# Gate and up projection computed as one pair, with seven block products in place of eight for three of eight k-tile pairs

## The chip, the cores and the metric

The kernel runs on one core of a Trainium2 chip. The metric is device microseconds for one execution of the whole program. TensorE (PE in the profile) does the matmuls into PSUM, VectorE (DVE), ScalarE (ACT) and GpSimd (POOL) do the rest, and SyncE (SP) issues nearly all DMAs. Each engine runs its own instructions in a fixed order and waits on semaphores for the others.

## The reference, cut to what matters

Two layers over 256 tokens of width 2048: a gated linear attention layer and a differential attention layer, each followed by the same feed-forward block. The change touches the feed-forward block and how the residual `x` is kept while it runs.

```
def swiglu(h, w_gate_up, w_down):                 # h: 256 x 2048
    gate, up = jnp.split(h @ w_gate_up, 2, axis=-1)   # 2048 x (2 * 5632)
    return (jax.nn.silu(gate) * up) @ w_down          # 5632 x 2048
x = x + rmsnorm(mix, post_mix_g[i])
f = swiglu(rmsnorm(x, pre_ffn_g[i]), ffn_w_gate_up[i], ffn_w_down[i])
x = x + rmsnorm(f, post_ffn_g[i])
```

Everything is float32.

## The kernel before, in words

**Matmuls.** A float32 operand is split into a rounded `hi` part and a remainder `lo`, and a product of 128 x 128 by 128 x 512 is three matmuls, hi by hi, hi by lo and lo by hi (`mm_act`, lines 220 to 222). The stationary operand is 128 columns of one half of the tokens (b = 0 or 1), the moving operand 512 weight columns.

**Weights.** They come in units of 128 x 1024 floats (512 KB): two k-tiles by 512 columns. `weight_stream` lists every unit in the order of use. `load` issues the DMA of one into a ring of 4 `raw` buffers (SP queue, line 174). `convert` makes `hi` by a copy on ACT (line 185) and `lo` by a subtraction on DVE (line 188), into rings of 9 buffers. `take` hands a unit to the matmuls, `free` returns it, and `pump` converts and loads ahead as far as the rings allow, so that DVE stands up to 9 units ahead of PE.

**Chunks.** `chunk_act` computes 512 output columns for 256 tokens: 8 units, two accumulators in PSUM (one for each half of the tokens), 12 matmuls per unit. PSUM has 8 banks; the pool `acc` has six and the pool `tp` (for transposes) two. Of 11 column chunks of the feed-forward block each has a gate chunk and an up chunk; gate ends in a SiLU on ACT (line 684), up in a multiply on DVE (line 687), and `split_T` transposes the result through `tp` (line 289) and splits it into `gT` (lines 291, 292). The 11 chunks go in groups of 3, 4 and 4; after a group, four down chunks accumulate into `f`.

**Order.** Python code with deferred steps (`defer`, `tick`) writes a program, and the framework's scheduler then fixes each engine's order from its own estimate of when each instruction becomes ready.

Of the kernel before, what the change touches and what calls it, by code (L numbers as in the profile page):

```python
# [11 lines left out]
F32 = mybir.dt.float32  # L12
# [24 lines left out]
LAMBDA_INIT = 0.8 - 0.6 * math.exp(-0.3 * 1)  # L37
FF_GROUPS = ((0, 1, 2), (3, 4, 5, 6), (7, 8, 9, 10))
SKEW = 7
CHAIN = (3, 4, 5, 6)  # L40
NRAW, NRING = 4, 9


def weight_stream():
    out = []

    def chunk(name, n, ns=8, s0=0):
        out.extend((name, (n, s0 + s)) for s in range(ns))

    def block(name, n):  # L50
        out.extend((name, (n, s)) for s in range(2))

    def ffn(i):
        for grp in FF_GROUPS:
            for c in grp:
                chunk(f"w_gu{i}", c)
                chunk(f"w_gu{i}", 11 + c)
# [24 lines left out]
    return out  # L82


class Split:

# [11 lines left out]
    def lo(self, kt, sl=slice(None)):  # L98
        return self.part(kt, 1, sl, 1)[:, 0, :]

    def both(self, kt):
        return self.tiles[kt // 8][:, kt % 8, :, :].rearrange("p w t -> p (w t)")


class Trunk:
    def __init__(self, ctx, tc, t):
# [12 lines left out]
        self.later = []  # L119
        self.stream = weight_stream()  # L120
        self.subs = {}
        self.raws = {}
# [48 lines left out]
    def load(self):  # L171
        name, idx = self.stream[self.n_dma]
# [3 lines left out]
        self.n_dma += 1  # L176

    def convert(self):
        nc = self.nc
        n = self.n_conv  # L180
        if self.n_dma == n:
            self.load()
        raw = self.raws.pop(n)
        hi = self.ring.tile([P, 1024], F32R, tag="hi", name=self.uid("hi"), bufs=NRING)
        nc.scalar.copy(hi, raw)  # L185
        lo = self.ring.tile([P, 1024], F32R, tag="lo", name=self.uid("lo"), bufs=NRING)
        eng = nc.gpsimd if n in self.pool_lo else nc.vector
        eng.tensor_tensor(out=lo, in0=raw, in1=hi.bitcast(F32), op=ALU.subtract)  # L188
        self.subs[n] = (hi, lo)
        self.n_conv += 1  # L190

    def pump(self):
        n = len(self.stream)
        while self.n_conv < min(n, self.n_free + NRING, self.n_take + self.cap):
            self.convert()
            while self.n_dma < min(n, self.n_conv + NRAW):
                self.load()

    def take(self, name, idx):
        n = self.n_take  # L200
        assert self.stream[n] == (name, idx), (self.stream[n], name, idx)
        self.n_take += 1
# [21 lines left out]
    def chunk_act(self, aT, w, n, ns, evac, s0=0, head=0, tail=0, hook=None):  # L224
# [32 lines left out]
        evac(1, ps[1])  # L257

    def block_w(self, aT, w, n, evac):
# [55 lines left out]
    def gain(self, vec, c):  # L315
        g = self.hs.tile([P, C], F32, tag="gain", name=self.uid("gain"), bufs=3)
        self.nc.sync.dma_start(g, vec[:, c * C : (c + 1) * C].partition_broadcast(P))
        return g
# [217 lines left out]
    def gla(self, gp, hT, rs):  # L536
        nc, t = self.nc, self.t
        self.wf = gp.tile([GATE_RANK, GLA_DK], F32, tag="wf", name="wf")
# [4 lines left out]
        s3 = self.whole(3, [P, 8, C], "gla_qk")  # L543

        def r_chunk(h, hook=None):
# [127 lines left out]

    def ffn(self, fp, hT, rs, gi, wgu, wd, post, after, name, side=None):
        nc = self.nc
        f = self.whole(5, [P, 2, D], name)
        ss = [self.stat(), self.stat()]
        for gidx, grp in enumerate(FF_GROUPS):
            gT = self.pair(gi, f"{name}_gT{gidx}")
            for i, c in enumerate(grp):  # L680
                sg = fp.tile([P, 2, C], F32, tag="sg", name=self.uid("sg"), bufs=2)

# [7 lines left out]

                first = gidx == 0 and i == 0
                if side and gidx == 1 and i == 0:
                    self.defer(8, side)
                self.chunk_act(hT, wgu, c, 8, evac_gate, head=SKEW if first else 0)
                self.chunk_act(hT, wgu, 11 + c, 8, evac_up)
# [5 lines left out]
                self.defer(3, gate_T)  # L701
            last = gidx == len(FF_GROUPS) - 1
            for c in range(4):
                g = self.gain(post, c) if last else None

                def evac(b, ps):
# [5 lines left out]
                    if last:  # L712
                        self.square(fc, ss[b][:, c : c + 1])
                        fg = fp.tile([P, C], F32, tag="fg", name=self.uid("fg"), bufs=2) if c == 3 else fc
                        nc.vector.tensor_tensor(out=fg, in0=fc, in1=g, op=ALU.mult)
                        if c == 3:
                            fgs = [f[:, b, i * C : (i + 1) * C] for i in range(3)] + [fg]
                            after(b, self.add_norm(fgs, b, ss[b]))

                self.chunk_act(  # L720
                    gT, wd, c, 2 * len(grp), self.urgent(evac) if last and c == 3 else evac, s0=2 * grp[0], tail=SKEW if last and c == 3 else 0
                )

    def diff_stages(self, dp, oT, q, kT, v, h):
# [60 lines left out]
        def normed():  # L785
            ctx["og"] = []
            for b, (o, ss) in enumerate(ctx["o"]):
                og = dp.tile([P, SEQ], F32, tag=f"og{b}", name=f"og{h}_{b}")
                nc.vector.scalar_tensor_tensor(
# [29 lines left out]
    def run(self):  # L819
# [5 lines left out]
        with tc.tile_pool(name="gla", bufs=1) as gp:  # L825
            oT = self.gla(gp, hT, rs)
            hT = self.pair(0, "h_ffn0")
            rs = []
            self.proj_out(
                oT, "gla_w_out", t["post_mix_g"][0:1],  # L830
                self.norm_to(hT, 1, rs, "rs_ffn0_"), "f_mix0",
            )

        x_dram = self.dram.tile([2, P, D], F32, tag="x_dram", name="x_dram")
        hkv, rs_kv = [], []
        with tc.tile_pool(name="ffn0", bufs=1) as fp:
# [7 lines left out]

            self.ffn(fp, hT, rs, 1, "w_gu0", "w_d0", t["post_ffn_g"][0:1], after, "f_ffn0", self.setup_diff)

        with tc.tile_pool(name="diff", bufs=1) as dp:
# [55 lines left out]
        with tc.tile_pool(name="ffn1", bufs=1) as fp:
# [95 lines left out]
```

## Time and profile before

| | |
|---|---|
| median of 3 runs | 2270.62 us (2270.39 to 2271.09) |
| profiled execution | 2271.46 us |
| its span, first to last instruction | 2269.7 us |
| PE busy | 2248.5 us, 10490 matmuls |
| DVE busy | 1245.1 us, 1501 instructions |
| ACT busy | 1072.6 us |
| DMA | 429.93 MB, mean 189 GB/s |

The busy shares are averages over the whole program. What decides here is how full PE and DVE are within the stretch of one gate and up pair, so the stretches are read one by one.

### The profile page before, as it was taken

Reading aid. Unit: us, or ns where it says so; the run is one execution under the profiler, and the core shown is the slowest. Engines: PE = TensorE matmul, PEld = TensorE weight load, DVE = VectorE, ACT = ScalarE, POOL = GpSimd, SP = SyncE. Lnnn points to the kernel's source line nnn. Section 1 sums busy time; section 2 is a strip of 40 time slices with the busy share of each in tenths; the row PEclk is TensorE's granted clock in tenths of the full one; section 3 lists DMA queues with packets and bytes.
Section 4 is the critical chain, followed back from the end, with each engine's and each line's share of the span. In section 5 each row is a group of like instructions: output and inputs, shape, how many; then the busy total and the mean of one; then the engine's idle time right before and its main releaser. Section 6 shows DMA issues by size and latency. Waiting matters only on the chain.

```text
span 2269.7 us, 27432 instructions
## 1 busy us (share of the span) xinstructions
PE 2248.5 (99%) x10490; PEld 1870.9 (82%) x10490; DVE 1245.1 (55%) x1501; ACT 1072.6 (47%) x1444; POOL 36.7 (2%) x68
## 2 busy tenths in 40 slices
PE   8999999999999999999999999999999999999998
PEld 7887888888888888888878888888888888888886
DVE  6864554754454554555575567656444454545454
ACT  7654444644444434444465445546444444344442
POOL 2000000000000000000000000000000000000000
PEclk9999999999999999999999999999999999999999
DMA  8555555666666666666575655556666666666663
GB/s 289 161 179 178 175 178 180 208 187 191 193 217 190 187 194 194 193 187 191 181 245 178 186 180 158 191 183 201 189 191 193 190 192 186 193 195 186 187 198 101
DMA packets 121976, 429.93 MB, mean 189 GB/s; under 512 B 13755, under 2 KB 16484, under 8 KB 121332
## 3 DMA queue, kind: packets, MB, share of 16 engines
q1 hardware_dynamic: 120812, 426.61, 60.9%
q8 instruction: 82, 1.34, 0.2%
q10 hardware_dynamic: 1032, 1.57, 0.2%
q14 instruction: 50, 0.41, 0.1%
HBM read 423.92 MB, written 5.78 MB: 189 GB/s over the span
## 4 chain that ended last, share of the span: by engine, by line
PE 95%; DMA 2%; DVE 1%; issue 1%; ACT 1%; POOL 0%; SPq 0%; DVEq 0%; POOLq 0%; ACTq 0%
PE acc L222 27%; PE acc L220 26%; PE acc L221 26%; PE acc L268 8%; PE acc L269 4%; PE tp L289 1%; DVE lo L188 0%; PE acc L738 0%; PE acc L777 0%; PE tp L324 0%; DVE x_in L356 0%; ACT junk L313 0%; PE acc L522 0%; DMA wf<-in_gla_w_fgate_dram 0%; DMA x_in<-in_x_dram 0%
## 5 line engine op out<-in xcount | busy, mean ns | idle before, releaser
L188 DVE TENSOR_TENSOR lo<-raw,hi 128x1024 fp32r<-128x1024 f32 x782 | 958.4, 1228 | 907.2 <-ACT hi L185 906.3
L185 ACT CAST hi<-raw 128x1024 fp32r<-128x1024 f32 x786 | 826.5, 1054 | 1003.8 <-PE acc L222 874.6
L222 PE MATMUL acc<-hi,h_ffn 128*128 128x512 f32 x1408 | 548.0, 390 | 2.7 <-DVE h_ffn L330 2.7
L220 PE MATMUL acc<-hi,h_ffn 128*128 128x512 f32 x1408 | 549.4, 390 | 0.0
L221 PE MATMUL acc<-lo,h_ffn 128*128 128x512 f32 x1408 | 548.1, 389 | 0.0
L222 PEld LDWEIGHTS acc<-hi,h_ffn 128*128 128x128 f32 x1408 | 264.2, 188 | 57.7 <-DVE h_ffn L330 3.1
L220 PEld LDWEIGHTS acc<-hi,h_ffn 128*128 128x128 f32 x1408 | 264.4, 188 | 54.7 <-issue 0.6
L221 PEld LDWEIGHTS acc<-lo,h_ffn 128*128 128x128 f32 x1408 | 264.3, 188 | 54.5
L220 PE MATMUL acc<-hi,f_ffn_gT 128*128 128x512 f32 x704 | 274.5, 390 | 0.0
L221 PE MATMUL acc<-lo,f_ffn_gT 128*128 128x512 f32 x704 | 274.0, 389 | 0.0
L222 PE MATMUL acc<-hi,f_ffn_gT 128*128 128x512 f32 x704 | 273.9, 389 | 0.0
L222 PEld LDWEIGHTS acc<-hi,f_ffn_gT 128*128 128x128 f32 x704 | 132.1, 188 | 27.6
L221 PEld LDWEIGHTS acc<-lo,f_ffn_gT 128*128 128x128 f32 x704 | 132.2, 188 | 27.2
L220 PEld LDWEIGHTS acc<-hi,f_ffn_gT 128*128 128x128 f32 x704 | 132.2, 188 | 27.0
L220 PE MATMUL acc<-hi,h_mix 128*128 128x512 f32 x256 | 101.9, 400 | 0.0
L221 PE MATMUL acc<-lo,h_mix 128*128 128x512 f32 x256 | 100.7, 393 | 0.0
L222 PE MATMUL acc<-hi,h_mix 128*128 128x512 f32 x256 | 100.2, 391 | 0.0
L268 PE MATMUL acc<-h_mix,hi 128*128 128x512 f32 x272 | 98.0, 403 | 0.0
L268 PE MATMUL acc<-h_q,hi 128*128 128x512 f32 x256 | 92.4, 401 | 0.0
L268 PE MATMUL acc<-h_kv,hi 128*128 128x512 f32 x256 | 90.6, 399 | 0.0
L269 PE MATMUL acc<-h_mix,lo 128*128 128x256 f32 x272 | 77.0, 283 | 0.0
L269 PE MATMUL acc<-h_q,lo 128*128 128x256 f32 x256 | 73.1, 286 | 0.0
(178 smaller groups left out, 2022.6 us busy)
## 6 DMA issues: line engine op xcount, KB each, us to landing
raw<-in_w_gu_dram SPq DMA_DIRECT2D x352, 512.0 KB, 3.8
raw<-in_w_d_dram SPq DMA_DIRECT2D x176, 512.0 KB, 3.6
raw<-in_gla_w_r_dram SPq DMA_DIRECT2D x32, 512.0 KB, 3.5
raw<-in_gla_w_v_dram SPq DMA_DIRECT2D x32, 512.0 KB, 3.6
raw<-in_gla_w_out_dram SPq DMA_DIRECT2D x32, 512.0 KB, 3.6
raw<-in_w_v_dram SPq DMA_DIRECT2D x32, 512.0 KB, 4.5
raw<-in_w_k_dram SPq DMA_DIRECT2D x32, 512.0 KB, 3.5
raw<-in_diff_w_q_dram SPq DMA_DIRECT2D x32, 512.0 KB, 3.6
```

The lines of the kernel that those rows point to most:

```text
L185: nc.scalar.copy(hi, raw)
L188: eng.tensor_tensor(out=lo, in0=raw, in1=hi.bitcast(F32), op=ALU.subtract)
L220: nc.tensor.matmul(ps, ah, rh, start=(kt == 0), stop=False)
L221: nc.tensor.matmul(ps, ah, rl, start=False, stop=False)
L222: nc.tensor.matmul(ps, al, rh, start=False, stop=(kt == 2 * ns - 1))
L268: nc.tensor.matmul(ps, lh, aT.both(kt), start=(kt == 0), stop=False)
L269: nc.tensor.matmul(ps[:, SEQ:], ll, aT.hi(kt), start=False, stop=(kt == KT - 1))
L289: nc.tensor.transpose(tp[:, j, :], src[:, j * P : (j + 1) * P], self.ident)
```

## The change

All gate and up pairs but the first of each layer are computed together, as a "duo". For a pair of k-tiles the product is a 2 x 2 by 2 x 2 block product: token halves by k-tiles, times k-tiles by (gate, up). For three of the eight pairs of k-tiles (`FAST`) it is done with seven products of sums and differences in place of eight. In the other five, eight products stay, one of them with the difference of the token halves. The seven results live in seven PSUM banks (six of `acc`, one of `tp`) over the whole duo, and VectorE combines them at its end. The sums of weights are made on VectorE as each pair is loaded; the sums of activations once per layer (`build_forms`), in the SBUF of the residual `x`, which is therefore written to DRAM before and read back ahead of the last down chunks. Groups are now 2, 3, 3 and 3 chunks.

```
-FF_GROUPS = ((0, 1, 2), (3, 4, 5, 6), (7, 8, 9, 10))
+FF_GROUPS = ((0, 1), (2, 3, 4), (5, 6, 7), (8, 9, 10))
+FAST = (0, 3, 6)
-NRAW, NRING = 4, 9
+NRAW, NRING = 5, 9
...
+    def duo(name, n1, n2):
+        for s in range(8):
+            if s in FAST:
+                out.extend((name, (n1, n2, s), kind) for kind in ("a", "c", "d", "b"))
+            else:
+                out.append((name, (n1, s), "plain"))
+                out.append((name, (n2, s), "plain"))
...
+    def split(self, src, pool=False):
+        nc = self.nc
+        w = src.shape[-1]
+        tag, bufs = ("", NRING) if w == 1024 else ("5", 1)
+        hi = self.ring.tile([P, w], F32R, tag="hi" + tag, name=self.uid("hi"), bufs=bufs)
+        nc.scalar.copy(hi, src)
+        lo = self.ring.tile([P, w], F32R, tag="lo" + tag, name=self.uid("lo"), bufs=bufs)
+        eng = nc.gpsimd if pool else nc.vector
+        eng.tensor_tensor(out=lo, in0=src, in1=hi.bitcast(F32), op=ALU.subtract)
+        return hi, lo
+    def sums(self):
...
+        add(r1[:, :C], r1[:, :C], r2[:, :C])
+        add(r2[:, :C], r2[:, :C], r2[:, C:])
+        add(t2, r1[:, :C], r2[:, C:])
+        add(r1[:, C:], t2, r1[:, C:])
+        self.pending = r1, r2, t2
     def convert(self):
...
+        self.n_done += kind in ("plain", "c", "b")
+        if kind == "plain":
+            self.subs[n] = self.split(self.raw(), n in self.pool_lo)
+        elif kind == "a":
+            self.pending = self.raw(), self.raw()
+            self.subs[n] = self.split(self.pending[0])
+        else:
+            if kind == "c":
+                self.sums()
+            self.subs[n] = self.split(self.pending["cbd".index(kind)])
...
+    def triple(self, ps, a, w, j, first, last):
+        nc = self.nc
+        ah, al = a
+        wh, wl = (t[:, j * C : (j + 1) * C] for t in w)
+        nc.tensor.matmul(ps, ah, wh, start=first, stop=False)
+        nc.tensor.matmul(ps, ah, wl, start=False, stop=False)
+        nc.tensor.matmul(ps, al, wh, start=False, stop=last)
+    def duo_act(self, aT, forms, w, n1, n2, early, late):
+        ps = [self.acc() for _ in range(6)] + [self.tp().rearrange("p j t -> p (j t)")]
+        for s in range(8):
+            k1, k2 = 2 * s, 2 * s + 1
+            if s in FAST:
+                f = FAST.index(s)
+                plan = {
+                    "a": ((0, (k1, 0)), (1, (k2, 0))),
+                    "c": ((4, (f, 0)), (3, (k2, 1))),
+                    "d": ((5, (f, 1)),),
+                    "b": ((6, (f, 2)), (2, (f, 3))),
+                }
...
+                        self.triple(ps[bank], a, wp, j, first, stop)
...
+            for n, pair in ((n1, ((1, 0), (3, 1))), (n2, ((4, 1), (2, 2)))):
+                wp = self.take(w, (n, s))
+                for bank, which in pair:
+                    for j in range(2):
+                        a = forms.diff(k1 + j) if which == 2 else aT.tokens(k1 + j, which)
+                        self.triple(ps[bank], a, wp, j, False, s == 7 and j == 1)
...
+        def fast_step(i):
...
+            op(r, hi, lo, ALU.add)
+            a11, a21, a12, a22 = (r[:, k, b * P : (b + 1) * P] for k in range(2) for b in range(2))
+            op(v[:, 2, :], a11, a21, ALU.subtract)
+            op(v[:, 0, :], a21, a22, ALU.subtract)
+            op(v[:, 1, :], v[:, 2, :], a22, ALU.add)
+            op(v[:, 3, :], a12, v[:, 1, :], ALU.subtract)
+            split(tuple(fast[:, i, p, :, :] for p in range(2)), v)
+        def diff_step(k, n):
...
+                op(out, a, b, ALU.subtract)
+            op(u, u, v, ALU.add)
+            split(tuple(d[:, at : at + n, p, :] for p in range(2)), u)
...
+        def early(ps):
+            made.extend((new_sg(), self.scratch(), self.scratch()))
+            sg, v, x = made
+            nc.scalar.copy(sg[:, 0, :], ps[0])
+            op(v, ps[5], sg[:, 0, :], ALU.subtract)
+            op(x, ps[6], v, ALU.subtract)
+        def late(bank, ps):
+            sg, v, x = made
+            if bank == 1:
+                op(sg[:, 0, :], ps[1], sg[:, 0, :], ALU.add)
+                nc.scalar.activation(sg[:, 0, :], sg[:, 0, :], AF.Silu, scale=rs[0])
+            elif bank == 3:
+                op(sg[:, 1, :], ps[3], x, ALU.add)
+                nc.scalar.activation(sg[:, 1, :], sg[:, 1, :], AF.Silu, scale=rs[1])
+            elif bank == 4:
+                op(x, ps[4], x, ALU.subtract)
+                op(v, ps[4], v, ALU.add)
+                gated(1, x)
+            else:
+                op(v, ps[2], v, ALU.add)
+                gated(0, v)
...
-                self.chunk_act(hT, wgu, c, 8, evac_gate, head=SKEW if first else 0)
+                self.chunk_act(hT, wgu, c, 8, evac_gate, head=SKEW)
+                for j, step in enumerate(steps):
+                    self.defer(2 * j + 1, step)
...
+            if last:
+                reload()
...
+            def stored(b, xs, norm=norm):
+                norm(b, xs)
+                self.defer(4, lambda: nc.sync.dma_start(x_mix0[b], self.x[:, b, :]))
+        def reload(src, name):
+            self.x = self.whole(4, [P, 2, D], name)
+            for b in range(2):
+                nc.sync.dma_start(self.x[:, b, :], src[b])
```

Smaller edits: the ring of `gain` vectors has 2 buffers in place of 3, `wf` lies in a tile that is there anyway, and two scratch tiles take other buffers.

In the orders below, `lo` is a conversion on DVE, `acc` and `tp` are PSUM banks, `hs` and `sg` the tiles in which a pair's result is put together. The first place is DVE at the end of a pair in the first layer, where one pair follows another. Before:

```order
L188 TENSOR_TENSOR lo_901_5125<-raw_890_5055,hi_900_5123 128x1024
L188 TENSOR_TENSOR lo_904_5143<-raw_893_5073,hi_903_5141 128x1024
L687 SCALAR_TENSOR_TENSOR sg_851_4839<-acc_883_5019,rs_ffn0_0_3462,sg_851_4839 128x512
L687 SCALAR_TENSOR_TENSOR sg_851_4839<-acc_884_5020,rs_ffn0_1_3567,sg_851_4839 128x512
L188 TENSOR_TENSOR lo_907_5163<-raw_896_5091,hi_906_5161 128x1024
L188 TENSOR_TENSOR lo_913_5184<-raw_899_5109,hi_912_5182 128x1024
L292 TENSOR_TENSOR f_ffn0_gT1_0_4837<-tp_915_5194,f_ffn0_gT1_0_4837 128x4x128
L292 TENSOR_TENSOR f_ffn0_gT1_0_4837<-tp_916_5201,f_ffn0_gT1_0_4837 128x4x128
```

Now, at the end of a duo (banks 1, 3, 4 and 2 of the old duo are `acc_1175`, `acc_1177`, `acc_1178` and `acc_1176`):

```order
L241 TENSOR_TENSOR lo_1245_6691<-raw_1226_6604,hi_1244_6689 128x1024
L850 TENSOR_TENSOR sg_1241_6667<-acc_1175_6363,sg_1241_6667 128x512
L850 TENSOR_TENSOR sg_1241_6667<-acc_1177_6365,hs_1243_6669 128x512
L241 TENSOR_TENSOR lo_1248_6714<-raw_1231_6632,hi_1247_6712 128x1024
L850 TENSOR_TENSOR hs_1243_6669<-acc_1178_6366,hs_1243_6669 128x512
L850 TENSOR_TENSOR hs_1242_6668<-acc_1178_6366,hs_1242_6668 128x512
L251 TENSOR_TENSOR raw_1231_6632<-raw_1231_6632,raw_1234_6644 128x512
L854 SCALAR_TENSOR_TENSOR sg_1241_6667<-hs_1243_6669,rs_ffn0_1_3573,sg_1241_6667 128x512
L850 TENSOR_TENSOR hs_1242_6668<-acc_1176_6364,hs_1242_6668 128x512
L251 TENSOR_TENSOR raw_1234_6644<-raw_1234_6644 128x512
L251 TENSOR_TENSOR sum_1256_6729<-raw_1231_6632,raw_1234_6644 128x512
L854 SCALAR_TENSOR_TENSOR sg_1241_6667<-hs_1242_6668,rs_ffn0_0_3468,sg_1241_6667 128x512
```

Two reads of PSUM at the end of a pair have become five, mixed with two multiplies and with conversions and sums for a unit that PE uses much later. The second place is PE at the same spot, a few matmuls into the next duo, whose banks 1, 4 and 3 are `acc_1250`, `acc_1253` and `acc_1252`:

```order
L347 MATMUL acc_1250_6717<-hi_1232_6640,h_ffn0_0_2641 128x512
L345 MATMUL acc_1250_6717<-hi_1238_6661,h_ffn0_0_2641 128x512
L346 MATMUL acc_1250_6717<-lo_1239_6663,h_ffn0_0_2641 128x512
L347 MATMUL acc_1250_6717<-hi_1238_6661,h_ffn0_0_2641 128x512
L345 MATMUL acc_1253_6720<-hi_1224_6600,f_ffn0_forms_3371 128x512
L346 MATMUL acc_1253_6720<-lo_1225_6602,f_ffn0_forms_3371 128x512
L347 MATMUL acc_1253_6720<-hi_1224_6600,f_ffn0_forms_3371 128x512
L345 MATMUL acc_1252_6719<-hi_1224_6600,h_ffn0_0_2641 128x512
```

The scheduler has pulled matmuls of later units (`hi_1232`, `hi_1238`) ahead of those of unit `hi_1224`: bank 4 is first written 18 matmuls after the old duo's last one. The third place is DVE where it makes the sums of a fast pair:

```order
L241 TENSOR_TENSOR lo_1222_6581<-raw_1203_6483,hi_1221_6579 128x1024
L251 TENSOR_TENSOR raw_1203_6483<-raw_1203_6483,raw_1209_6516 128x512
L251 TENSOR_TENSOR raw_1209_6516<-raw_1209_6516 128x512
L251 TENSOR_TENSOR sum_1223_6595<-raw_1203_6483,raw_1209_6516 128x512
L251 TENSOR_TENSOR raw_1203_6483<-sum_1223_6595,raw_1203_6483 128x512
L241 TENSOR_TENSOR lo_1225_6602<-raw_1203_6483,hi_1224_6600 128x1024
L241 TENSOR_TENSOR lo_1230_6630<-raw_1209_6516,hi_1229_6628 128x1024
```

The conversion `lo_1225` stands right behind the fourth sum, and it needs `hi_1224`, which ACT can only make from that sum. So it stands in 36 of the 60 fast pairs; in the other 24 one or more instructions lie between.

## Rows read from the trace of the kernel before

**Rows 1.** The page's part 1: busy time of each engine
```profile
PE 2248.5 (99%) x10490; PEld 1870.9 (82%) x10490; DVE 1245.1 (55%) x1501; ACT 1072.6 (47%) x1444; POOL 36.7 (2%) x68
```

**Rows 2.** The page's part 4: the chain that ended last, by engine
```profile
PE 95%; DMA 2%; DVE 1%; issue 1%; ACT 1%; POOL 0%; SPq 0%; DVEq 0%; POOLq 0%; ACTq 0%
```

**Rows 3.** The chain in order of time, one pair apart: start us, us, what
```profile
500.24 0.87 PE tp L289 x8
...
544.65 0.87 PE tp L289 x8
```

**Rows 4.** Busy time by stretch: the pair between those transposes
```profile
core 0: us, PE busy (x) PEld busy (x) DVE busy (x) ACT busy (x) POOL busy (x), PEclk, DMA share, GB/s
...
500.24:544.65 44.41, 44.41 (x202) 36.87 (x201) 22.22 (x21) 19.22 (x20) 0.00 (x0) 1.00 0.62 190
```

**Rows 5.** Timeline of PE: start us, us, instruction; eleven rows lie between
```profile
464.71 0.39 PE L220 MATMUL acc<-hi,h_ffn 128*128 128x512 f32 x1
...
467.43 0.39 PE L220 MATMUL acc<-hi,h_ffn 128*128 128x512 f32 x1
```

**Rows 6.** Groups by line and form, DVE and ACT: busy us, mean ns, idle
```profile
L188 DVE TENSOR_TENSOR lo<-raw,hi 128x1024 fp32r<-128x1024 f32 x782 | 958.4, 1228 | 907.2 <-ACT hi L185 906.3
L185 ACT CAST hi<-raw 128x1024 fp32r<-128x1024 f32 x786 | 826.5, 1054 | 1003.8 <-PE acc L222 874.6 <-PE acc L268 96.7 <-DMA raw<-in_w_gu_dram 15.1
...
L687 DVE SCALAR_TENSOR_TENSOR sg<-acc,rs_ffn,sg 128x512 f32<-128x512 f32 x44 | 30.9, 743 | 0.0
...
L292 DVE TENSOR_TENSOR f_ffn_gT<-tp,f_ffn_gT 128x512 fp32r<-128x512 f32 x44 | 28.4, 687 | 17.3 <-ACT f_ffn_gT L291 17.3
...
L711 DVE TENSOR_TENSOR f_ffn<-acc,f_ffn 128x512 f32<-128x512 f32 x32 | 20.7, 683 | 21.2 <-PE acc L222 21.2
...
L715 DVE TENSOR_TENSOR f_ffn<-f_ffn,gain 128x512 f32<-128x512 f32 x12 | 7.9, 684 | 0.0
...
L281 DVE TENSOR_TENSOR q<-acc,hs 128x256 f32<-128x256 f32 x16 | 6.7, 418 | 0.0
...
L343 DVE TENSOR_SCALAR hs<-ident,rs_mix 128x128 f32<-128x128 f32 x2 | 0.6, 284 | 0.5 <-POOL rs_mix L308 0.5
```

**Rows 7.** Timeline of DVE, instructions that follow each other without a wait
```profile
397.75 4.63 DVE L188 TENSOR_TENSOR lo<-raw,hi 128x1024 fp32r<-128x1024 f32 x4
...
495.02 1.40 DVE L687 SCALAR_TENSOR_TENSOR sg<-acc,rs_ffn,sg 128x512 f32<-128x512 f32 x2
...
501.33 1.29 DVE L292 TENSOR_TENSOR f_ffn_gT<-tp,f_ffn_gT 128x512 fp32r<-128x512 f32 x2 [0.79 <-ACT f_ffn_gT L291]
```

**Rows 8.** Timeline of ACT: the copy of a unit
```profile
481.91 1.05 ACT L185 CAST hi<-raw 128x1024 fp32r<-128x1024 f32 x1 [1.67 <-PE acc L222]
```

**Rows 9.** Timeline of DVE: the subtraction that waits for that copy
```profile
483.00 1.22 DVE L188 TENSOR_TENSOR lo<-raw,hi 128x1024 fp32r<-128x1024 f32 x1 [1.49 <-ACT hi L185]
```

**Rows 10.** Timeline of DVE: an instruction that reads the result of the last
```profile
58.50 0.69 DVE L455 TENSOR_TENSOR hs<-hs,hs 128x512 f32<-128x512 f32 x1 [0.72 <-ACT hs L450]
59.23 1.22 DVE L456 TENSOR_TENSOR_SCAN hs<-scan_mask,hs 128x512 f32<-128x512 f32 x1
```

**Rows 11.** Waits of PE, whole span: us in total, times, longest us
```profile
PE acc L222 <- DVE h_ffn L330: 2.7, 2, 1.4
PE acc L222 <- DVE h_kv L330: 1.6, 1, 1.6
```

**Rows 12.** Page, parts 3 and 6: share of the DMA engines; us to landing
```profile
q1 hardware_dynamic: 120812, 426.61, 60.9%
...
raw<-in_w_gu_dram SPq DMA_DIRECT2D x352, 512.0 KB, 3.8
```

**Rows 13.** DMA issues: the residual read back, as before does it once
```profile
x_mid<-x_dram SPq DMA_DIRECT2D x2, 1024.0 KB, 7.7
```

**Rows 14.** The chain in order of time, at the start of the program
```profile
9.92 6.81 DMA wf<-in_gla_w_fgate_dram
16.81 5.02 DMA raw<-in_gla_w_r_dram
```

More of the change, by code (lines that the diff above doesn't have):

```diff
@@ L82, in weight_stream, with load_list @@
     return out
+def load_list(stream):
+    out = []
+    for name, idx, kind in stream:
+        if kind == "plain":
+            out.append((name, idx))
+        elif kind == "a":
+            n1, n2, s = idx
+            out.extend([(name, (n1, s)), (name, (n2, s))])
+    return out
 class Split:
@@ L99, in lo, with tokens, __init__, fast @@
         return self.part(kt, 1, sl, 1)[:, 0, :]
+    def tokens(self, kt, b):
+        sl = slice(b * P, (b + 1) * P)
+        return self.hi(kt, sl), self.lo(kt, sl)
     def both(self, kt):
         return self.tiles[kt // 8][:, kt % 8, :, :].rearrange("p w t -> p (w t)")
+class Forms:
+    def __init__(self, fast, diff):
+        self.f, self.d = fast, diff
+        self.plain = [k for k in range(KT) if k // 2 not in FAST]
+    def fast(self, i, which):
+        return tuple(self.f[:, i, p, which, :] for p in range(2))
+    def diff(self, kt):
+        d, i = self.place(kt)
+        return tuple(d[:, i, p, :] for p in range(2))
+    def place(self, kt):
+        i, n = self.plain.index(kt), self.d[0].shape[1]
+        return (self.d[0], i) if i < n else (self.d[1], i - n)
 class Trunk:
@@ L176, in load, with raw, add @@
         self.n_dma += 1
+    def raw(self):
+        if self.n_dma == self.n_used:
+            self.load()
+        self.n_used += 1
+        return self.raws.pop(self.n_used - 1)
+    def split(self, src, pool=False):
[10 more added lines that the diff above has]
+        nc = self.nc
+        r1, r2 = self.pending
+        t2 = self.ring.tile([P, C], F32, tag="sum", name=self.uid("sum"), bufs=1)
+        def add(out, in0, in1):
+            nc.vector.tensor_tensor(out=out, in0=in0, in1=in1, op=ALU.add)
+        add(r1[:, :C], r1[:, :C], r2[:, :C])
[3 more added lines that the diff above has]
+        self.pending = r1, r2, t2
     def convert(self):
-        nc = self.nc
         n = self.n_conv
[L181 to L189, printed above, removed]
+        kind = self.stream[n][2]
+        self.n_done += kind in ("plain", "c", "b")
+        if kind == "plain":
+            self.subs[n] = self.split(self.raw(), n in self.pool_lo)
+        elif kind == "a":
+            self.pending = self.raw(), self.raw()
[4 more added lines that the diff above has]
+            self.subs[n] = self.split(self.pending["cbd".index(kind)])
         self.n_conv += 1
@@ L257, in chunk_act @@
         evac(1, ps[1])
+    def triple(self, ps, a, w, j, first, last):
+        nc = self.nc
+        ah, al = a
[15 more added lines that the diff above has]
+                }
+                first, last = s == FAST[0], s == FAST[-1]
+                for kind, prods in plan.items():
+                    wp = self.take(w, (n1, n2, s), kind)
+                    for j, (bank, (i, which)) in enumerate(prods):
+                        plain = kind == "a" or bank == 3
+                        a = aT.tokens(i, which) if plain else forms.fast(i, which)
+                        stop = last and bank in (0, 5, 6)
+                        self.triple(ps[bank], a, wp, j, first, stop)
+                    self.free()
+                    if kind != "d":
+                        self.tick()
+                if last:
+                    early(ps)
+                continue
+            for n, pair in ((n1, ((1, 0), (3, 1))), (n2, ((4, 1), (2, 2)))):
[4 more added lines that the diff above has]
+                        self.triple(ps[bank], a, wp, j, False, s == 7 and j == 1)
+                    if s == 7:
+                        late(bank, ps)
+                    if bank in (2, 3):
+                        self.free()
+                    self.tick()
@@ L702, in ffn @@
             last = gidx == len(FF_GROUPS) - 1
+            if gidx == 0:
+                f = self.whole(5, [P, 2, D], name)
+                if side:
+                    self.defer(20, side)
+            if last:
+                reload()
             for c in range(4):
```

115 lines of the change are left out of this document (81 added, 34 removed).

## The prediction, made before the changed kernel had run

> **What bounds the kernel now.** I read the busy table first: PE is busy 2248.5 of 2269.7 us, DVE 55% [rows 1]. A busy PE need not be a full one, so the chain that ended last comes next: 95% of it is PE, and nothing else has more than 2% [rows 2]. So only PE time counts, unless another engine grows until it bounds a stretch. The stretch that the change rebuilds is a gate and up pair. In the chain its transposes come back after 544.65 - 500.24 = 44.41 us [rows 3]; in that stretch PE has no gap, at a granted clock of 1.00, the upper level of 2.4 GHz, and DVE works 22.22 us, half of it [rows 4]. The pair has 2 x 8 units x 12 = 192 matmuls and 8 transposes (0.87 us). A matmul's row lasts 390 ns, but twelve start within 467.43 - 464.71 = 2.72 us, so each costs PE 226.7 ns [rows 5], and 192 x 0.2267 + 0.87 = 44.4 is the pair.
>
> **What it removes.** A duo has 5 x 24 + 3 x 21 = 183 matmuls: nine fewer, 2.04 us, so a duo that PE bounds takes 42.37 us. There are 10 duos in each layer, 180 matmuls fewer in all: -40.8 us. The stationary operand still changes at each matmul and the moving one still has 512 columns, so I keep 226.7 ns.
>
> **What it adds on DVE, the term that decides.** Per duo, by whole rows [rows 6]:
> - conversions: 10 plain units and 3 x 3 fast ones of 1024 columns, 19 x 1.228 = 23.3; three of 512 at 0.684 (the SBUF row of that width): 2.1
> - sums of weights: 12 x 0.684 = 8.2
> - reading seven banks: 7 x 0.683 = 4.8; two multiplies 1.5; two splits of the transposes 1.4
>
> Together 41.2 us, where the pair before had 22.2. But rows overlap: four conversions without a wait take 4.63 us, so one costs (4.63 - 1.228) / 3 = 1.134; two splits take 1.29, so one of 512 costs 1.29 - 0.687 = 0.60; two multiplies take 1.40, 0.66 each [rows 7]. At these: 21.5 + 1.8 + 7.2 + 4.2 + 1.3 + 1.2 = 37.3. Two things come on top. The conversion of unit c waits for the ACT copy of what the fourth sum wrote: the copy takes 1.05 and DVE starts 0.04 after it [rows 8, 9], some 1.1 us idle in the 36 fast pairs where it stands right behind that sum, and about 0.4 in the other 24, 0.8 on average, 2.5 per duo. And an instruction that reads its predecessor's result starts only 0.04 after that one's end [rows 10], 0.13 later than in the overlapped case: some ten per duo, 1.3. Sum: 41.1 us of DVE for 42.4 of PE. DVE goes from half full to 97%, and still fits, by 1.3 us per duo. Between the groups 16 to 24 down units (12 matmuls, 2.72 us each, for one conversion of 1.134) let it catch up.
>
> An average that fits can still starve PE locally. In a fast pair DVE needs 4 x 0.60 + 0.3 + 0.8 + 3 x 1.134 + 0.60 = 7.5 us for 21 x 0.2267 = 4.8 of PE; a plain pair gives back 5.44 - 2.27 = 3.2. The worst run is at a duo's end: fast pair -2.7, plain pair +3.2, banks and multiplies -5.5, next fast pair -2.7, so DVE falls some 8 us back. Of the duo's 22 units 9 are converted ahead, 9/22 x 42.4 = 17 us, so PE doesn't run out of weights. What it can meet is a bank not yet read: DVE's order holds the reads behind conversions for 9 units ahead. The order gives it room: bank 4 gets its last product 6 matmuls before the old duo ends and is first written 18 after, 24 x 0.2267 = 5.4 us for two reads of 0.6; bank 1 has 18 + 3 matmuls, 4.8 us, for one read. So DVE may be about 4 us late before PE stands. Where PE meets a long DVE chain in a fixed order now, at the layer boundaries, it waits 1.3 to 1.6 us [rows 11]. Bounds per duo: nothing (the room holds) and 1.6; I take 0.3, nearer to the room, 6 us over 20 duos.
>
> **Other terms.**
> - Making the activation forms: per layer three fast steps (2 x 0.684 + 4 x 0.28) and five differences (4 x 0.418), 7.5 + 8.4 = 16 us of DVE, with the rows of 256 and 128 columns [rows 6]. They lie beside the first up chunk (21.8 us of PE, where eight conversions need 9.1) and into the first duo, which has 1.3 us to spare. Over chunk and duo DVE is short by 16 - 12.7 - 1.3 = 2 us, and the ring holds more; between 0 and 5 us per layer I take 2: 4 us.
> - ACT: at most 19.2 + 3 x 1.05 + four copies of 512 under 1.05 each = 27 of 42.4 us; hidden [rows 4, 6].
> - The residual: two MB out and two back per layer, 8 MB on 430, with the DMA engines at 60.9% [rows 12]. The read back takes 7.7 us [rows 13]; it stands in SP's queue ahead of down units while up to 9 converted units, 24 us, lie ready. If that cover were gone it would cost those 7.7 us per layer. The store waits on SP for DVE's residual add, and the raw loads behind it feed ACT's copies some ten units later; nothing. The shorter `gain` ring waits for reads a chunk earlier: nothing. A fourth group adds 8 reads (5.5 us of DVE) per layer, in down stretches where DVE is half idle.
> - The start: two loads stand on the chain there, `wf` (6.81) and behind it a unit (5.02) [rows 14]. One more unit is now loaded ahead of `wf`, and one `gain` load less stands before the rest. Between 0 and -5 us; I take -2.
>
> Sum: -40.8 + 6 + 4 - 2 = -32.8. The profiled execution took 2271.46 (span 2269.7 and 1.8 around it), 0.84 above the median, so 2238.7 there and **2238 us** on the median's scale. With all stalls at their lower bound it is 2225 to 2230, at their upper ones (32 + 10) 2272, but only if every boundary waits as long as the worst one now; I set the likeliest case's own range at 2229 to 2252.
>
> **The rivals.**
> - *DVE becomes the bound.* If whole rows don't overlap as they do in a short run of four, a duo costs 41.2 + 2.5 = 43.7 us, 1.35 more than PE: 27 us back, and with the other 8 the time is 2270.6 - 40.8 + 27 + 8 = 2265. For it: 97% on a strictly ordered engine with waits for ACT, PE and DMA in its queue. Against: the rows of runs without a wait, and the down stretches.
> - *The banks stall PE (slower).* The pair before used two of six accumulators at a time, so a bank was read while others filled. A duo holds seven of eight through its whole length, and the next needs the same ones at once. If DVE reaches the reads late, PE stands at each duo's start, however many units lie converted. The point from which it decides is 2.04 us per duo, the nine matmuls saved. Three conversions too many ahead of the reads, beyond the room, are 3.4 us: 20 x 3.4 = 68 less 40.8, some 2298; half of it ends level. Against: the 4 us of room in PE's order.
>  On this the Trainium skill (Perfetto Trace Analysis, Optimizing Tensor Performance, Matmuls) says that independent groups of matmuls should rotate through PSUM banks so that one group's evacuation overlaps the next group's matmuls. By that rule the change takes away what hid the reads, and the time would be this rival's; the trace of before, with a pair end without any gap on PE, agrees that rotation hides them, and cannot show the other case.
> - *Nothing stalls and the start gains.* 2270.6 - 40.8 - 5 = 2225.
> - *The fast products don't pay per matmul* (a changed cost of one with forms as the stationary operand): excluded as far as the rows go, since 226.7 ns holds for every operand pair; it is part of the slower case.
>
> **How the numbers follow.** What a measurement of this kernel can tell from no change is 0.2%, 4.5 us: 2266 to 2275. Likeliest case 0.62; nothing stalls 0.07; DVE bound 0.18, of which 0.13 ends below 2266 and 0.05 in the band; banks 0.13, slower. So faster 0.62 + 0.07 + 0.13 = 0.82, same 0.05, slower 0.13. The range leaves out the slower case and the band (0.18) and part of the best one: 2227 to 2266.
>
> **What the profile after would show.** Matmul count 180 lower at 226.7 ns apart. Inside a group of three, duos 42.4 us apart between transposes: right if 42.4 to 43; DVE bound if nearer 44 with PE waiting for `lo` of DVE in all of the duo; banks if PE's waits sit at the first products of banks 1, 4 and 3 behind the reads of the old duo, over 1 us each. DVE busy about 41 us per duo, ACT about 25. Idle of DVE behind the fourth sum near 1 us, waiting for ACT. PE waits for DVE of 2 us in each layer's first duo. No wait of PE or ACT for the residual's DMA. Wrong would be a mean gap above 0.8 us per duo, or a matmul spacing other than 226.7 ns.

## The result, and the profile after

The changed kernel takes **2241.45 us** (median of 4 runs, 2241.26 to 2242.42), the kernel before 2270.51 in the same measurement (2269.64 to 2271.09): a ratio of 0.9873, 95% interval 0.9856 to 0.9890. Forecast were 2238 us, 2227 to 2266. The time is 3.5 us off, but the sum holds 10 us of stalls that did not come and lacks some 12 us that did.

The page of the kernel after, its busy line and its chain by engine, answer to [rows 1, 2]:

```profile
PE 2210.2 (99%) x10310; PEld 1835.3 (82%) x10310; DVE 1605.4 (72%) x2093; ACT 1166.4 (52%) x1602; POOL 38.9 (2%) x68
...
PE 97%; DVE 1%; ACT 1%; issue 1%; DMA 0%; POOL 0%; SPq 0%; DVEq 0%; POOLq 0%; ACTq 0%
```

10490 - 10310 = 180 matmuls fewer, as counted, and PE is still nearly the whole chain. To see where the 29 us went I take the same four events from both traces. These are PE's instructions by line and tile: count, duration (ns: least, median, most), start of the first and of the last. Before:

```profile
L220 PE MATMUL acc<-hi,h_ffn x1408: 387/389/501, 402.9 to 2172.2; 128*128 128x512 f32 x176
L268 PE MATMUL acc<-h_kv,hi x256: 391/398/478, 1232.8 to 1323.3; 128*128 128x512 f32 x128
L220 PE MATMUL acc<-hi,diff_oT x128: 387/389/578, 1434.5 to 1527.7; 128*128 128x512 f32 x128
L220 PE MATMUL acc<-hi,f_ffn_gT x704: 387/389/482, 539.7 to 2260.2; 128*128 128x512 f32 x176
```

After:

```profile
L302 PE MATMUL acc<-hi,h_ffn x128: 387/389/478, 399.8 to 1565.8; 128*128 128x512 f32 x128
L438 PE MATMUL acc<-h_kv,hi x256: 390/398/479, 1211.0 to 1301.5; 128*128 128x512 f32 x128
L302 PE MATMUL acc<-hi,diff_oT x128: 387/389/586, 1421.5 to 1518.8; 128*128 128x512 f32 x128
L302 PE MATMUL acc<-hi,f_ffn_gT x704: 387/389/501, 489.3 to 2230.4; 128*128 128x512 f32 x176
```

| from | to | before | after | difference |
|---|---|---|---|---|
| start | first `h_ffn` | 402.9 | 399.8 | -3.1 |
| first `h_ffn` | first `h_kv` block: feed-forward, layer 1, and `w_v` | 829.9 | 811.2 | -18.7 |
| there | last `diff_oT`: the attention heads | 294.9 | 307.8 | **+12.9** |
| there | last `f_ffn_gT`: feed-forward, layer 2 | 732.5 | 711.6 | -20.9 |

The two feed-forward blocks gave 39.6 us, nearly the whole price of 180 matmuls (40.8). The attention heads, which the change seemed not to touch, took 12.9 back. The chain there, after (start us, us, what), shows one head after another:

```profile
1319.02 1.31 PE acc L968 x8
...
1331.82 1.29 PE acc L1007 x6
1333.12 1.31 PE acc L968 x8
...
1346.01 1.04 ACT hi L238
...
1347.33 0.39 ACT aT L1000
1347.76 1.56 PE acc L1007 x6
1349.32 1.31 PE acc L968 x8
```

From the second head on ACT stands in the chain, and a head takes 1349.32 - 1333.12 = 16.2 us. The product with v (line 1007) waits for the copy `aT`. PE's waits in the whole span (us in total, times, longest us) name the same copy; they answer to [rows 11]:

```profile
PE acc L1007 <- ACT aT L1000: 7.9, 6, 1.3
PE tp L494 <- DMA x_in<-in_x_dram: 6.9, 2, 4.2
PE acc L304 <- DVE h_kv L500: 3.4, 2, 2.3
```

Two more, of 1.2 and 1.1 us for `diff_oT`, come just before the last of these six: with them PE waits 10.2 us for what the heads make. No wait stands at lines 345 to 347, the matmuls of the duos: neither weights nor banks held PE up in any of the twenty.

### The profile page after: what moved, and what is told of

Same layout as the page of the kernel before. It is cut to its first block, busy times and chain, and to the rows that moved or that the text cites. A ratio compares the mean times of both kernels' runs of the same rounds, so it can differ in the third digit from the quotient of the medians.

```text
span 2239.9 us, 28021 instructions
## 1 busy us (share of the span) xinstructions
PE 2210.2 (99%) x10310; PEld 1835.3 (82%) x10310; DVE 1605.4 (72%) x2093; ACT 1166.4 (52%) x1602; POOL 38.9 (2%) x68
## 3 DMA queue, kind: packets, MB, share of 16 engines
q1 hardware_dynamic: 121964, 434.99, 57.9%
## 4 chain that ended last, share of the span: by engine, by line
PE 97%; DVE 1%; ACT 1%; issue 1%; DMA 0%; POOL 0%; SPq 0%; DVEq 0%; POOLq 0%; ACTq 0%
PE acc L304 14%; PE acc L302 14%; PE acc L303 14%; PE acc L347 12%; PE acc L345 12%; PE acc L346 12%; PE acc L438 8%; PE acc L439 4%; PE tp L459 1%; PE tp L494 1%; PE tp L347 1%; PE tp L345 1%; PE tp L346 1%; PE acc L1007 1%; DVE lo L241 0%
## 5 line engine op out<-in xcount | busy, mean ns | idle before, releaser
L241 DVE TENSOR_TENSOR lo<-raw,hi 128x1024 fp32r<-128x1024 f32 x842 | 1013.7, 1223 | 513.1 <-ACT hi L238 509.7
L238 ACT CAST hi<-raw 128x1024 fp32r<-128x1024 f32 x846 | 873.4, 1052 | 830.6 <-PE acc L304 375.5
L346 PE MATMUL acc<-lo,h_ffn 128*128 128x512 f32 x780 | 304.3, 390 | 0.0
L347 PE MATMUL acc<-hi,h_ffn 128*128 128x512 f32 x780 | 304.1, 390 | 0.0
L345 PE MATMUL acc<-hi,h_ffn 128*128 128x512 f32 x780 | 303.9, 390 | 0.0
L302 PE MATMUL acc<-hi,f_ffn_gT 128*128 128x512 f32 x704 | 274.8, 390 | 0.0
L345 PEld LDWEIGHTS acc<-hi,h_ffn 128*128 128x128 f32 x780 | 146.4, 188 | 30.5
L347 PEld LDWEIGHTS acc<-hi,h_ffn 128*128 128x128 f32 x780 | 146.5, 188 | 30.4
L346 PEld LDWEIGHTS acc<-lo,h_ffn 128*128 128x128 f32 x780 | 146.5, 188 | 30.2
L302 PEld LDWEIGHTS acc<-hi,f_ffn_gT 128*128 128x128 f32 x704 | 132.2, 188 | 27.8 <-issue 0.6
L302 PE MATMUL acc<-hi,h_mix 128*128 128x512 f32 x256 | 102.1, 400 | 0.0
L347 PE MATMUL acc<-hi,f_ffn_forms 128*128 128x512 f32 x260 | 101.8, 392 | 0.0
L345 PE MATMUL acc<-hi,f_ffn_forms 128*128 128x512 f32 x260 | 101.8, 392 | 0.0
L346 PE MATMUL acc<-lo,f_ffn_forms 128*128 128x512 f32 x260 | 101.2, 389 | 0.0
```

The lines of the kernel that those rows point to most:

```text
L238: nc.scalar.copy(hi, src)
L241: eng.tensor_tensor(out=lo, in0=src, in1=hi.bitcast(F32), op=ALU.subtract)
L302: nc.tensor.matmul(ps, ah, rh, start=(kt == 0), stop=False)
L345: nc.tensor.matmul(ps, ah, wh, start=first, stop=False)
L346: nc.tensor.matmul(ps, ah, wl, start=False, stop=False)
L347: nc.tensor.matmul(ps, al, wh, start=False, stop=last)
```

## The experiments

All were timed beside the kernel before (2271.0 to 2271.4 us there).

**The heads.** The suspect is an edit that the change lists among the smaller ones. `normed` no longer writes a head's output `og` into a tile of its own but into the scores' tile `s`, which has one buffer for all heads. A head takes 8 ticks; the scores of the next are due 3 ticks into it, the transposes of `og` at tick 14 of the old one, so 6 into the next.

```
+            pair = self.const.tile([P, 2, SEQ], F32, tag="scan_mask", name=f"og{h}")
             for b, (o, ss) in enumerate(ctx["o"]):
-                og = ctx["s"][1][0][:, b, :]
+                og = pair[:, b, :]
```

> The changed kernel with one edit: the normalised head output og gets a buffer of its own again (the 2 kB of the scan mask, dead by then), where the change had put it into the scores' tile s. Theory 'shared buffer': the attention heads lost 13.6 us because the next head's scores can be written into s only when this head's output has been transposed out of it. Then this run takes 2228 us (2241.5 - 13.6), 2227 to 2231, and the wait of the att_v matmuls for the copy aT (7.9 + 9.3 us) goes below 2 us in all. Rival 'the rest of the change' (five raw tiles, another order of the weight ring, the residual's DMA, hi conversions ahead of the copy): the time stays at 2241 +- 2. If half, both have a part.

Measured: 2229.25 us (2228.52 to 2229.55), ratio 0.9816 (0.9801 to 0.9831), and PE has no wait for `aT` or `diff_oT` left. And the reverse, the kernel before with that edit alone:

```
-                og = dp.tile([P, SEQ], F32, tag=f"og{b}", name=f"og{h}_{b}")
+                og = ctx["s"][1][0][:, b, :]
```

> The kernel before with that one edit alone: og is written into the scores' tile s, nothing of the products or of the residual is changed. Theory 'shared buffer': the heads alone lose it, 2270.5 + 13.6 = 2284 us, 2281 to 2287. Rival 'the rest of the change': 2270.5 +- 2, since before has the old ring and the old queue.

Measured: 2283.93 us (2281.65 to 2284.67), ratio 1.0055 (1.0038 to 1.0072). The edit is worth 12.2 us one way and 12.9 the other, and in the second run PE's waits have the same row, of the same size, as after:

```profile
PE acc L777 <- ACT aT L770: 7.9, 6, 1.3
```

How it works shows in DVE's timeline around one head (start us, us, instruction, idle before it and what ended it). After:

```profile
1334.35 0.41 DVE L972 TENSOR_TENSOR s<-acc,bias 128x256 f32<-128x256 f32 x1
...
1335.14 0.96 DVE L1019 SCALAR_TENSOR_TENSOR s<-acc,st,subg 128x256 f32<-128x256 f32 x2
...
1339.76 0.69 DVE L972 TENSOR_TENSOR s<-acc,bias 128x512 f32<-128x512 f32 x1 [0.33 <-PE tp L1028]
```

With a buffer of its own:

```profile
1334.80 0.41 DVE L972 TENSOR_TENSOR s<-acc,bias 128x256 f32<-128x256 f32 x1
...
1335.19 0.68 DVE L972 TENSOR_TENSOR s<-acc,bias 128x512 f32<-128x512 f32 x1
```

The add that takes the next head's second scores out of PSUM comes 0.4 us after the first where `s` is free, and 5.4 us after it where `og` lies in `s` until PE (L1028) has transposed it. Softmax and combination of these scores follow 4 to 6 us late, and their transposes on PE start at 1346.00 in place of 1343.15. The copy `aT` then starts at 1347.23 in place of 1343.56, in ACT's fixed order behind a `hi` copy of 1.04 us. The head period is 14.5 us in the chain of the version with the buffer, as in the kernel before (1354.88 to 1369.38), and ACT is gone from the chain:

```profile
1333.57 1.31 PE acc L968 x8
...
1346.77 1.29 PE acc L1007 x6
1348.07 1.31 PE acc L968 x8
```

**Does anything stall at three pairs?** `FAST = (0, 6)` in place of `(0, 3, 6)`:

> The changed kernel with seven products in two k-tile pairs of eight (the first and the seventh) in place of three. PE has 3 matmuls more per duo, 60 in all, 60 x 0.2267 = +13.6 us; DVE has some 5 us less per duo. Theory 'PE bounds, nothing stalls at three': 2241.5 + 13.6 = 2255.1, within 1.5. Theory of the prediction, 0.3 us of stall per duo at three pairs and 1 to 2 us per layer from the forms: with DVE's load cut these 6 + 2 us come back, 2247 to 2250. DVE as the bound would make it as fast as or faster than three of eight.

Measured: 2256.27 us (2255.93 to 2256.97), 14.8 us more than after, against 13.6 for the 60 matmuls. Nothing came back: the duos did not stall at three.

**How much room has DVE?** In `sums`, the third sum made three times:

```
         add(t2, r1[:, :C], r2[:, C:])
+        add(t2, r1[:, :C], r2[:, C:])
+        add(t2, r1[:, :C], r2[:, C:])
```

> The changed kernel with the third sum of weights made three times in place of once (the same result again, on DVE): 6 more instructions of 512 columns per duo at a pitch of 0.60, 3.6 us of DVE per duo, 72 us in all, nothing for PE. Theory of the prediction: DVE has 1.3 us to spare per duo, so 2.3 us per duo are too many; over 20 duos 46 us, less what the down stretches make up: 2256 to 2287. Rival: the profile after has DVE at 38.3 us busy in a duo of 43.4, its idle time is nearly all in front of conversions, and the down stretches follow each three duos: the extra fits, 2241.5 to 2244.

Measured: 2242.19 us (2241.91 to 2243.11), 0.7 more than after. And five times:

> The changed kernel with the third sum made five times: 12 more instructions of 512 columns per duo at 0.60, 7.2 us of DVE per duo. DVE then needs 38.3 + 7.2 = 45.5 us in a duo of 42.4. Theory 'each duo pays': 3.1 x 20 = 62 us, 2304. Theory 'the converted units lying ahead pay first': three duos of a group fall 9.3 us back, the lead is 9 units or 17 us, and the down stretches refill it; then 2242 to 2252. If it costs nothing at all, DVE's room is larger than its busy time says.

Measured: 2299.32 us (2298.61 to 2300.54), 57.9 more, close to 62. But not each duo pays. PE's waits, and a stretch of the first group of three duos (us, busy us of each engine, granted clock, DMA):

```profile
PE acc L349 <- ACT hi L238: 36.2, 6, 6.6
```

```profile
620.00:624.00 4.00, 2.59 (x12) 1.81 (x10) 4.00 (x7) 1.45 (x2) 0.00 (x0) 1.00 0.13 53
624.00:628.00 4.00, 0.00 (x0) 0.00 (x0) 3.96 (x7) 0.56 (x1) 0.00 (x0) 0.83 0.00 0
628.00:632.00 4.00, 2.82 (x7) 2.24 (x8) 3.58 (x5) 3.97 (x6) 0.00 (x0) 0.50 0.15 29
```

PE waits six times, once in each group of three duos, where DVE's lateness has used up the units that lay ready. So the lead pays first, as the second theory said, but its price was far too low: six waits of 6 us, and in each the clock falls to 0.50, its lower level, and stays there when PE goes on. PE is busy 17.9 us longer than after for the same matmuls (2228.1 against 2210.2).

The extra sums had also let the scheduler put the conversion of unit d into DVE's idle time behind the fourth sum, which the changed kernel does in 17 of 60 fast pairs only (42 with two more sums, 50 with four). So a second load was put elsewhere, three plain units per duo converted twice:

```
+            if name[:4] == "w_gu" and 0 < idx[0] < 11 and idx[1] in (1, 2, 4):
+                hi, lo = self.subs[n]
+                self.nc.vector.tensor_tensor(out=lo, in0=raw, in1=hi.bitcast(F32), op=ALU.subtract)
```

> The changed kernel with three plain units of each duo converted twice on DVE (the second lo overwrites the first with the same values): 3 x 1.134 = 3.4 us of DVE per duo. More sums had also moved the conversion of unit d into DVE's idle time behind the fourth sum (the conversion of unit c stands right behind it in 36 of 60 fast pairs of the changed kernel, in 10 with two more sums, in none with four more); here it stays there in 30. Theory of the prediction (a duo needs 41.1 us of DVE in the changed kernel's own order, idle time behind the sum included): 44.5 for 42.4, 2.1 us per duo, 6.3 per group of three; four more sums were 3.0 per duo over and PE waited 6 us once per group, so 3 of 9 were covered; here 6.3 - 3 = 3.3 x 6 groups = 20 us and half as much again at the lower clock, 2258 to 2272. Rival (a duo needs 38.2, so 4.2 are free): 41.6, it fits, 2241.5 to 2243.5.

Measured: 2242.53 us (2241.39 to 2243.02), 1.1 more. 3.4 us more per duo fit, with the idle time left in half of the pairs. This does not make 38.2 the exact need, since a deficit of 1 to 2 us per duo can also hide in the lead of a group; it shows that there was room for more than the prediction gave.

**Does a late read of a bank cost?** Before the read that counts, bank 1 is read 12 times, or 6, into a half of `sg` that is overwritten after:

```
             if bank == 1:
+                for _ in range(12):
+                    op(sg[:, 1, :], ps[1], sg[:, 0, :], ALU.add)
```

> The changed kernel with bank 1 read 12 more times (into a half of sg that is overwritten right after) before the read that counts: 7.2 us of DVE per duo as with four more sums, but all of it between the bank's last product and the next duo's first matmul into it, together with some six conversions that stand between. Theory 'the room of the banks': that matmul comes 21 x 0.2267 = 4.8 us after the last product, the last read ends 13 x 0.60 + 6 x 1.13 = 14.6 us after it; PE stands 9 to 10 us at every duo that follows a duo and somewhat more where a down stretch follows (bank 0 and 1 come first there): 20 x 9.8 = 196 less what the other reads gain, 2380 to 2440. Rival 'lateness of reads does not matter, only DVE's sum does': as with four more sums, 2242 to 2304.

> As the run with 12 more reads of bank 1, with 6: 3.6 us of DVE per duo as with two more sums, which cost 0.7 us in all. The last read ends 7 x 0.60 + 3 x 1.13 = 7.6 us after the last product, against 4.8 us of room. Theory 'the room of the banks': 2.8 us x 20 = 56, 2285 to 2305. Rival 'only DVE's sum matters': 2242 to 2243.

Measured: 2381.53 us (2377.93 to 2387.64) with 12 and 2285.99 (2284.96 to 2287.46) with 6. Both lie in the range of the bank theory, and the same six instructions per duo had cost 0.7 us as sums, so their place counts. But the waits bear the theory out only in part for 12 and not for 6. PE's waits with 12 more reads:

```profile
PE acc L302 <- DVE sg L850: 31.9, 8, 6.8
PE acc L345 <- DVE sg L850: 22.3, 12, 2.8
PE tp L345 <- ACT hi L238: 21.4, 6, 4.6
```

With 6:

```profile
PE tp L345 <- ACT hi L238: 16.4, 6, 2.7
...
PE acc L345 <- ACT hi L238: 6.6, 12, 0.8
...
PE acc L302 <- DVE sg L850: 0.4, 1, 0.4
```

With 12, 54.2 of 88 us of waits are for the read of a bank (DVE `sg`), at the next duo (L345) and at the next down chunk (L302): 20 waits of 2.7 us on average where the theory had 9.8. The time came into its range by 34 us of waits for weights and a longer busy PE (last section). With 6 the banks cost 0.4 us, and PE runs out of weights instead. DVE's timeline there:

```profile
623.77 0.68 DVE L850 TENSOR_TENSOR sg<-acc,sg 128x512 f32<-128x512 f32 x1
624.37 0.68 DVE L251 TENSOR_TENSOR raw<-raw,raw 128x512 f32<-128x512 f32 x1
624.97 0.68 DVE L850 TENSOR_TENSOR sg<-acc,sg 128x512 f32<-128x512 f32 x1
...
627.37 0.68 DVE L251 TENSOR_TENSOR raw<-sum,raw 128x512 f32<-128x512 f32 x1
```

and ACT and PE behind it:

```profile
628.14 2.94 ACT L238 CAST hi<-raw 128x1024 fp32r<-128x1024 f32 x3 [6.68 <-DVE raw L251]
```

```profile
630.18 0.79 PE L345 MATMUL tp<-hi,f_ffn_forms 128*128 128x512 f32 x1 [2.73 <-ACT hi L238]
```

The reads stand between the sums of the next fast pair; ACT idles 6.68 us for a sum, and PE 2.73 us for ACT's copy. So the place where DVE's lateness first hurts is the fourth sum of the pair after a duo's end, not the bank. The theory of the banks had the time for the run with 6 and not the place.

**Four pairs of eight**, with the separate buffer, and four raw tiles in place of five to make room for the table of differences:

> The changed kernel with the separate buffer of the earlier run (2229.25 us), and seven products in four k-tile pairs of eight (the first, third, fifth, seventh); to make room for the longer table of differences the raw tiles go from five to four. PE has 60 matmuls fewer, -13.6 us; DVE gets some 4.9 us more per duo (4 sums of 0.60, net conversions 1.7, 0.8 behind the fourth sum). Theory 'it still fits' (3.6 us more per duo fitted, and the converted units ahead cover a group of three duos): 2215.6, within 2. Theory 'DVE is the bound from here' (DVE at 38.3 of 43.4 us per duo, so 43.2 needed in 41.7): 1.5 us per duo and more, 2229 to 2246, no gain over three of eight.

Measured: 2248.47 us (2247.59 to 2249.63), 19.2 more than three pairs with that buffer, 32.8 above what PE alone would give. The size would fit DVE as the bound at 43.3 us per duo, though the time is 2.5 us above the range given for that. Two runs try it, by taking the unit d before c (`("a", "d", "c", "b")`), so that its conversion fills DVE's idle time, and by moving the second sum to GpSimd as well (`nc.gpsimd.tensor_tensor` for `r2[:, :C]`):

> Four pairs of eight (2248.47) with the order a, d, c, b. Theory 'DVE's idle time behind the fourth sum made it the bound': DVE needed 43.3 us per duo (41.7 of PE and 32.8 / 20 us of loss); filling that time in some half of the pairs takes 1.5 to 2 us off, so 41.3 to 41.8: 2216 to 2225. Rival 'four raw tiles or the reads of the banks are the cause': no change, 2246 to 2250.

> As the run with four pairs and order a, d, c, b, with the second of the four sums on GpSimd (only the last unit of the pair needs it; 1024 columns took 2.4 us there, so 512 some 1.2 by half). DVE has 4 x 0.60 = 2.4 us less per duo, 39 to 39.5 for 41.7 of PE. Theory 'DVE's work is the bound at four pairs': PE bounds again, 2214 to 2218. Rival: GpSimd's reads and writes beside DVE slow DVE or come late for the ACT copy of b: 2225 or more.

Measured: 2250.32 us (2249.0 to 2252.95) and 2269.92 (2266.63 to 2272.88). In the first, DVE's idle time right behind the fourth sums falls from 46 to 25 us in all, and the time did not fall, where the theory asked for 23 to 32 us less: that idle time is hardly the cause. The second does not test DVE's work, because it did not lessen it. DVE has 80 instructions fewer there and is busy 1708.0 us against 1692.6. Its fourth sum, which runs beside GpSimd's add, takes twice as long as in the changed kernel, and GpSimd's own add takes 1.72 us, not the 1.2 of the estimate (busy us, mean ns, idle; first the changed kernel, then the run with GpSimd):

```profile
L251 DVE TENSOR_TENSOR raw<-sum,raw 128x512 f32<-128x512 f32 x60 | 41.2, 687 | 1.4
```

```profile
L254 POOL TENSOR_TENSOR raw<-raw 128x512 f32<-128x512 f32 x80 | 137.7, 1721 | 1139.6 <-DVE raw L251 1120.7
...
L251 DVE TENSOR_TENSOR raw<-sum,raw 128x512 f32<-128x512 f32 x80 | 114.0, 1425 | 2.3
```

So the rival of that expectation came in its first half: DVE is slower beside GpSimd. The chain by engine of the run with four pairs:

```profile
PE 81%; DVE 7%; DMA 6%; ACT 4%; issue 1%; POOL 0%; SPq 0%; ACTq 0%; DVEq 0%; POOLq 0%
```

and of the run with the sum on GpSimd:

```profile
PE 59%; DVE 19%; DMA 14%; ACT 5%; issue 3%; POOL 0%; DVEq 0%; ACTq 0%; SPq 0%; POOLq 0%
```

The loads of raw tiles are in the chain, together with DVE and ACT: a load starts when a tile is free, and a fast pair holds two of the four until its sums are converted. That loop may be the cause. It is argued from the chain alone: four pairs with five raw tiles, or three pairs with four, did not run, so whether the tiles, the fourth pair or DVE's work makes the loss stays open.

**The order a, d, c, b with three pairs** and the separate buffer:

> The version with the separate buffer (2229.25), three pairs of eight, with the units of a fast pair taken in the order a, d, c, b in place of a, c, d, b: d needs only the third sum, so its conversion can fill DVE's idle time while ACT copies c (conversion of d behind the fourth sum in 42 of 60 pairs). Theory 'PE bounds with room': nothing changes, 2229.25 within 1.5. If DVE was close enough to cost PE something here, up to 6 us faster: 2223.

Measured: 2229.45 us (2228.62 to 2230.0): no change. With PE as the bound DVE's idle time is worth nothing. The two versions at 2229 are the best, 41.8 and 41.9 us under the kernel before beside them.

## Why the prediction was right or wrong

- **180 matmuls at 226.7 ns, -40.8: right.** The feed-forward blocks gave 39.6, with 1.8 more of waits at `h_kv` than before. In a duo of the kernel after, twelve matmuls start within 600.50 - 597.77 = 2.73 us, against 2.72 [rows 5]:

```profile
597.77 0.39 PE L346 MATMUL acc<-lo,h_ffn 128*128 128x512 f32 x1
...
600.50 0.39 PE L346 MATMUL acc<-lo,h_ffn 128*128 128x512 f32 x1
```

  Between transposes (586.55 and 629.91, stretch below) lie 43.36 us and not 42.4, outside the 42.4 to 43 that the prediction named, but 197 records. Two of them only reach in over the ends, as in the 202 for 200 before; that leaves four matmuls more than 183 and 8 transposes, 0.9 us: the transposes of the second duo stand four matmuls later.
- **DVE's work per duo: right in size.** The sum was 37.3 + 1.3 us of work and 2.5 us of idle time behind the fourth sum. Busy time of one duo, columns as in [rows 4]:

```profile
586.55:629.91 43.36, 43.36 (x197) 35.88 (x196) 38.29 (x47) 23.31 (x28) 0.00 (x0) 1.00 0.55 193
```

  38.29 against 38.6; ACT 23.3 where "about 25" was forecast. The idle time behind the fourth sum is 1.2 us, as worked out, where unit c's conversion stands there:

```profile
583.08 4.63 DVE L241 TENSOR_TENSOR lo<-raw,hi 128x1024 fp32r<-128x1024 f32 x4 [1.19 <-ACT hi L238]
...
607.76 3.50 DVE L241 TENSOR_TENSOR lo<-raw,hi 128x1024 fp32r<-128x1024 f32 x3 [1.17 <-ACT hi L238]
```

- **The stalls, 6 us for the duos and 4 for the forms: wrong, they were nothing.** "DVE may be about 4 us late before PE stands" and "fits, by 1.3 us per duo" were taken as if DVE's deficits came to PE one by one. The units lying ready cover a group of three duos: 3.4 and 3.6 us more per duo cost 1.1 and 0.7 us in all. Somewhere between 3.6 and 7.2 the lead is used up within a group; 7.2 cost 58 us. And the room at the banks was there: even six more reads ahead of the one that counts brought 0.4 us of waits for a bank. The predicted wait of PE in each layer's first duo isn't there either.
- **The start, -2: right**, -3.1.
- **The residual's DMA, ACT, the gain ring: right.** No wait of PE names them.
- **Two scratch tiles in other buffers: missed, +12.9.** The prediction has no term for them. One of the two put `og` into `s`, and since then the next head can write its scores only after the last read of this head's output: a free order became a chain. With that edit taken back the time is 2229.25 us, in the 2225 to 2230 that the prediction works out for stalls at their lower bound; its own rival for that, "nothing stalls", had a chance of 0.07.
- **The rivals.** DVE did not become the bound. The banks did not stall PE. The Trainium skill (Perfetto Trace Analysis, Optimizing Tensor Performance, Matmuls) says that groups of matmuls should rotate through PSUM banks, so that evacuation overlaps. The traces agree with it where the reads are made very late (54.2 us of waits for a bank with 12 more reads); in the changed kernel itself, where seven of eight banks are held, they show no such wait.

So 40.8 less was right, 10 us of stalls did not come, and 12.9 us came from a place that was not looked at. The time agreed by luck, because the two errors nearly cancel.

## What to carry to other kernels

Price every buffer that a change merges: ask when its last reader runs, and when the next writer wants it; here two kilobytes per partition cost 12 us, and a tile that had gone dead elsewhere gave them back. An engine that is full on the average of one step can still be hidden if another step lets it catch up and the units lying ready cover the time between; test it by adding work until it shows, and look at which wait appears, since the time alone fitted a wrong theory here: with six more reads of a bank PE hardly waited for a bank at all. And look whether an experiment did what it was meant to: work moved to GpSimd left DVE no less busy.

## What the runs showed that was not expected

A wait of PE can cost more than its length. With 6 more reads PE waits 2.73 us at 630.18, and the stretches around it show the clock (last three columns: granted clock, DMA share, GB/s):

```profile
626.00:630.00 4.00, 1.45 (x7) 0.87 (x5) 3.97 (x7) 1.86 (x2) 0.00 (x0) 0.95 0.09 37
630.00:634.00 4.00, 3.66 (x8) 2.58 (x9) 4.00 (x6) 2.41 (x4) 0.00 (x0) 0.50 0.53 139
634.00:638.00 4.00, 4.00 (x14) 3.15 (x13) 3.18 (x5) 0.00 (x0) 0.00 (x0) 0.70 0.71 253
```

It falls from 1.00 (2.4 GHz) to 0.50 (1.2 GHz) towards the end of the gap and comes back some 7 us later here, sooner behind some of the other waits. Over the whole run PE is busy 19.6 us longer than after (2229.8 against 2210.2) beside 24 us of waits: nearly as much again. With 12 more reads it is 55.2 us beside 88 of waits. The waits in the heads, 1.3 us at most, cost much less beside their length. Over the stretch of all heads in the kernel after the granted clock is 1.00 (0.99 in the kernel before with the shared tile):

```profile
1319.02:1449.90 130.88, 120.72 (x665) 103.05 (x664) 92.73 (x186) 70.14 (x158) 7.64 (x14) 1.00 0.48 159
```

PE is busy 120.7 us there against 118.0 in the version with the buffer, 2.7 us more beside 10.2 of waits.
